# Two more query tiles transposed outside TensorE, and softmax weights divided late, in a streaming encoder step

## The chip, the cores and the metric

The kernel runs on one core of a Trainium2 chip. A core has TensorE (PE, matmuls; its weight loads are shown apart as PEld), VectorE (DVE), ScalarE (ACT), GpSimd (POOL) and SyncE (SP), which in this kernel issues every DMA, in one queue. The metric is the device time of one execution in microseconds; the median of several runs counts.

## The reference, cut to what matters

One layer of an encoder for a prompt of 1024 tokens and a sample group of 32 tokens with a cache of 512, all in float32:

```python
def finish(h, oa, ga, ob, gb, w_out, g_post, p, w_ple, w_ple_gate):
    y = jnp.concatenate([oa * jax.nn.silu(ga), ob * jax.nn.silu(gb)], axis=-1) @ w_out
    h = h + rmsnorm(y, g_post)
    return h + jax.nn.sigmoid(h @ w_ple_gate) * (p @ w_ple)

def band_attention(q, k, v, q_pos, k_pos, bias_table):      # heads A: 8 heads of 64
    s = jnp.einsum('bqhd,bkhd->bhqk', q, k).astype(jnp.float32) * ATTN_SCALE
    s = s + bias_table[:, rel]
    s = jnp.where(ok, s, NEG_INF)             # own chunk of 64 and the 8 chunks before
    w = jax.nn.softmax(s, axis=-1)
    return jnp.einsum('bhqk,bkhd->bqhd', w, v)

def stick_breaking(q, k, v, q_pos, k_pos):                  # heads B: 8 heads of 64
    z = jnp.einsum('bqhd,bkhd->bhqk', q, k).astype(jnp.float32) * ATTN_SCALE
    log_beta = jax.nn.log_sigmoid(z)
    log_1m = jnp.where(causal, jax.nn.log_sigmoid(-z), 0.0)
    after = lax.cumsum(log_1m, axis=3, reverse=True) - log_1m
    w = jnp.where(causal, jnp.exp(log_beta + after), 0.0)
    return jnp.einsum('bhqk,bkhd->bqhd', w, v)
```

Queries, keys, values and gates of both kinds come from one projection, `rmsnorm(h) @ w_in`. With s(z) the sigmoid, the weight of heads B is s(z_k) times the product of s(-z_j) over all later keys j.

## The kernel before, in words

**Precision.** A float32 operand is split in a high part, rounded to the fast matmul format, and a low part, the rest. A product takes three fast matmuls (high x high, low x high, high x low).

**Stages.** Eight head pairs are worked on in the order A0, B0, A1, B1, A2, B2, A3, B3. While one pair's attention runs, the projections of the next pair are woven in: keys, queries, values, each in three chunks of 352 tokens (24 matmuls a chunk). Beside the last pair stand the eight gate projections `gA`, `gB`. After the attention come the input embedding (`ple`), the output projection (`o0P1`, `o1P1` and so on, seven products per group of row tiles), the norm, and the last gate (`g0P1` ...). Names with `s` (`sA`, `sB`) are the sample group.

**One head.** A head has eight query tiles of 128 rows, i = 0 to 7. Tile i of heads B reads i + 1 key blocks of 128, tile i of heads A at most 5.

- `scores(i)`: two matmuls per piece of at most 512 columns write the scores to PSUM (`SA`, `SB`). In heads B a mask is added, then ScalarE writes the sigmoid of the negated scores (`om`) and the sigmoid of the scores (`be`), VectorE turns `om` into reversed running products (TENSOR_TENSOR_SCAN), and POOL multiplies both. In heads A VectorE adds the bias (read reversed) and takes the row maximum, ScalarE writes the exponentials and their sum, VectorE inverts the sum, and POOL multiplies the weights by it.
- `weights_t(i)`: the weights are turned, blocks of 128 x 128, to keys by queries. By default PE transposes them (`ptwA`, `ptwB`), ScalarE rounds the result into the high ring (`wTh`), VectorE writes the rest into the low ring (`wTl`). `ROUND` names the tiles that go another way, 4 and 6 of heads A: VectorE transposes squares of 32 x 32, one DMA stores the tile to DRAM (`swapA`), four DMAs read it back so that the squares come to their places, and rounding and subtraction run from SBUF.
- `values(g)`: for the four tiles of group g, value matmuls (`PVA`, `PVB`) accumulate in one bank, with the turned weights as the operand that is streamed; `Segments` is its access pattern, with a run of 128 elements per query tile. Low and high value parts end in different partitions; ScalarE copies one half, VectorE adds the other, and a DMA stores `ot` to `o_dr`.

**Buffers.** `om` and `be` are two rings in SBUF (`Arena`), of 3076 and 3384 columns; `wTh` and `wTl` are two more of 33 blocks. A tile of a ring waits until the earlier users of its columns are done.

**Gates.** Each of 24 gate chunks is 24 matmuls, a sigmoid on ScalarE, a product on VectorE, a product on POOL with the attention output loaded from `o_dr` (`ogg`), and a store to `og_dr`, from which the output projection loads its left sides (`uo`, `lo`). Gate buffers `sg` are three.

**Order.** Nothing is issued where it is written: `Recorder` records every operation with its dependencies, and `order` lists them by a simulation with built-in costs, engine by engine; each engine then works through its list in order. On PE the attention has the better key, and projection matmuls fill in where it is not ready. All operations are issued from one line, so the profile shows line L450 nearly everywhere, and groups are told apart by tiles.

Of the kernel before, what the change touches and what calls it, by code (L numbers as in the profile page):

```python
# [30 lines left out]
ROUND = {"A": ((4,),(6,)), "B": ()}  # L31
# [127 lines left out]
class Segments:  # L159


    def __init__(self, buf, start, step, n):
        self.buf, self.start, self.step, self.n = buf, start, step, n
        self.shape = [buf.shape[0], n, P]
        self.box = (buf.box[0], (start, start + (n - 1) * step + P))

    def get(self):
        base = self.buf.get()[:, self.start:self.start + P]
        return bass.AP(tensor=base.tensor, offset=base.offset, ap=[base.ap[0], [self.step, self.n], [1, P]])
# [83 lines left out]

class Engine:
# [9 lines left out]
class Recorder:  # L264
# [43 lines left out]
    def add(self, eng, what, args, kw):  # L308
        writes, reads = [], []
        method = what[1] if isinstance(what, tuple) else ""  # L310
        for i, a in enumerate(args):
            if isinstance(a, (View, Raw, Segments)):
                (writes if i == 0 or (method == "tensor_tensor_reduce" and i == 7) else reads).append(a)
        for k, a in kw.items():
            if isinstance(a, (View, Raw, Segments)):
                (writes if k in ("out", "accum_out") else reads).append(a)
        o = self.node(eng, what, args, kw, set())
        for mine, write in ((reads, False), (writes, True)):
            for v in mine:
                b = v.buf  # L320
                hit = False
                for other, box, wrote in b.uses:
                    if other is not o and (write or wrote) and all(p < y and x < q for (p, q), (x, y) in zip(v.box, box)):
                        o.after.add(other)
                        hit = True
# [4 lines left out]
                b.uses.append((o, v.box, write))  # L330
        o.busy, o.late = self.cost(eng, method, args, kw, writes, reads)
        o.shared = eng == "POOL"
        if eng == "DVE":
            sbuf = [v for v in reads if isinstance(v, (View, Segments)) and not v.buf.psum and v.free() > 4]
            o.shared = len(sbuf) > 1 or (method == "tensor_copy" and len(sbuf) == 1 and not writes[0].buf.psum)

    @staticmethod
    def cost(eng, method, args, kw, writes, reads):
# [3 lines left out]
        psum = any(isinstance(v, (View, Segments)) and v.buf.psum for v in reads)  # L342
# [97 lines left out]
    def emit(self, tc):  # L440
        ops = self.order()
        with tc.manual_schedule():
            for o in ops:
# [3 lines left out]
                args = [a.get() if isinstance(a, (View, Raw, Segments)) else a for a in o.args]  # L447
                kw = {k: a.get() if isinstance(a, (View, Raw, Segments)) else a for k, a in o.kw.items()}
# [7 lines left out]
def stream_step(  # L456
# [22 lines left out]
    o_dr = [scratch([P, T], f"o_dr{n}") for n in range(8)]  # L479
# [34 lines left out]
    ring0, ring1 = Arena(rec, at, "om", 3076), Arena(rec, at, "be", 3384)  # L514
    ringh, ringl = (Arena(rec, at, x, 33 * P, F32R) for x in ("wTh", "wTl"))
# [10 lines left out]
    NAMES = ["qA", "kA", "vA", "gA", "qB", "kB", "vB", "gB"]  # L526

# [14 lines left out]
    def ensure(j):  # L542
# [6 lines left out]
        if j == 2:  # L549
            pair = [ringl.tile([P, 2, 4, P], f"w{x}_{kind}{p}") for x in "hl"]  # L550
# [14 lines left out]
    def load_x(t):  # L565
        n = min(P, T - t * P)
        if t == 3:
            x34.append(at.tile([P, ringh.cols], F32, tag="wTh", name="x34")[:, 0:2 * D].rearrange("p (a c) -> p a c", a=2))
# [37 lines left out]
    def bias_rows():  # L606

        rb = ring0.tile([8, 257], "rb")
        dma(rb, rel_bias[0])
        R = ring1.tile([8, 768], "R")  # L610
# [101 lines left out]
    def col_steps(j):  # L712
# [7 lines left out]
        def mms(c, part):  # L720
# [9 lines left out]
            if k == "g" and part == 0:  # L730
                box["og"] = at2.tile([P, CH], F32, tag="bias", name=f"og{kind}{p}_{c}", bufs=2)
                dma(box["og"], o_dr[n][:, cs])
# [8 lines left out]
            if k == "g":  # L741
# [3 lines left out]
                nc.gpsimd.tensor_tensor(sg, sg, box["og"], ALU.mult)  # L745
                dma(og_dr[n, :, cs], sg)
            elif k == "q":
                nc.scalar.activation(box["st"][:, cs], acc, AF.Copy, scale=SCALE)
# [28 lines left out]

    def attention(ab, p, h):
# [5 lines left out]
        def begin():  # L784
            if ab == "A":
                bias = at2.tile([P, 640], F32, tag="bias", name=f"bias{nm}", bufs=2)
                dma(bias, bias_src(2 * p + h, P, 0, 640))
                nc.gpsimd.memset(bias[0:HD, 0:HD], NEG)
                nc.gpsimd.memset(bias[HD:P, 576:640], NEG)
# [4 lines left out]

        together = {i: g for g in ROUND[ab] for i in g}
        whole, done_with = {}, []
# [4 lines left out]
        def rooms(i):  # L801

            more = ab == "B"
            g = together.get(i, (i,))
            if g not in whole:
                n = sum(cost(x) for x in g) * P
                whole[g] = ring0.tile([P, n + more * len(g)], f"om{nm}_{i}"), ring1.tile([P, n], f"be{nm}_{i}")
            k, n = g.index(i), cost(i) * P
            a = sum(cost(x) for x in g[:k]) * P
            w0, w1 = whole[g]  # L810
            return w0[:, a + more * k:a + more * k + n + more], w1[:, a:a + n]

        def scores(i):
# [5 lines left out]
            w0, w1 = rooms(i)  # L819
# [8 lines left out]
            if ab == "B":  # L828
# [3 lines left out]
                nc.gpsimd.memset(w0[:, n:n + 1], 1.0)  # L832
                for a, b, s in pieces:
                    nc.scalar.activation(w0[:, a:b], s, AF.Sigmoid, scale=-1.0)
                for a, b, s in pieces:
                    nc.scalar.activation(w1[:, a:b], s, AF.Sigmoid)
                for a, b, s in reversed(pieces):
                    rev = w0[:, a + 1:b + 1][:, ::-1]
                    nc.vector.tensor_tensor_scan(rev, rev, s, 1.0 if b == n else w0[:, b + 1:b + 2], ALU.mult, ALU.bypass)
                nc.gpsimd.tensor_tensor(w1[:, 0:n], w1[:, 0:n], w0[:, 1:n + 1], ALU.mult)  # L840
            else:
                m = small.tile([P, 4], F32, tag="stat", name=f"stat{nm}_{i}", bufs=6)
                for j, (a, b, s) in enumerate(pieces):
                    nc.vector.tensor_tensor_reduce(
                        w0[:, a:b], s, box["bias"][:, n - b:n - a][:, ::-1], 1.0,
                        -3e38 if j == 0 else m[:, j - 1:j], ALU.add, ALU.max, m[:, j:j + 1])
                last = len(pieces) - 1
                nc.vector.tensor_scalar(m[:, 2:3], m[:, last:last + 1], -1.0, None, ALU.mult)
# [3 lines left out]
            state[i] = w0, w1  # L852

        wT = {}
# [5 lines left out]
        def weights_t(i):  # L860
            g = i // 4
            step, size = LAID[ab, g]
            if g not in wT:
                wT[g] = [x.tile([P, size * P], f"{x.name}{nm}_{g}") for x in (ringh, ringl)]
            b0 = lo_block(i)
            w0, w1 = state.pop(i)
            n = i + 1 - b0
            at_ = ((i - 4 * g) * step + b0) * P
            hi, lo = (x[:, at_:at_ + n * P] for x in wT[g])
            if i in together:  # L870

                group = together[i]
                done_with.append((i, hi, lo))
                if i != group[-1]:
                    return
                w0, w1 = whole[group]
                m = sum(cost(x) for x in group)
                first = {x: sum(cost(y) for y in group[:k]) for k, x in enumerate(group)}
                squares = w0[:, 0:m * P].rearrange("p (c b q) -> p b c q", c=4, q=32)
                for x, _, _ in done_with:  # L880
                    y = slice(first[x], first[x] + cost(x))
                    nc.vector.transpose(squares[:, y], w1[:, y.start * P:y.stop * P])
                dr = scratch([P, m * P], f"swap{nm}_{i}")
                dma(dr, w0[:, 0:m * P])
                for c in range(4):
                    x = dr[:, c * m * 32:(c + 1) * m * 32].rearrange("(g k) x -> k g x", k=32)
# [964 lines left out]
```

## Time and profile before

| | |
|---|---|
| median of 3 runs | 806.26 us (805.87 to 806.33) |
| span of the profiled execution | 802.6 us; the median is 3.7 us above it |
| PE busy | 792.0 us, 4734 matmuls |
| PEld busy | 731.4 us |
| DVE busy | 565.7 us |
| ACT busy | 539.5 us |
| POOL busy | 469.5 us |
| DMA | 146.32 MB, 61.3% of 16 engines' span |

Matmuls overlap, and their ends are modelled; the distance from one start to the next tells what a matmul costs on a full engine. In the lines by stretch the columns are PE, PEld, DVE, ACT and POOL busy time with instruction counts, the granted clock, the DMA share and GB/s. A group's line gives busy time, the mean of one in ns, and the idle time of the engine ahead of it with what ended it. A DMA group's line ends with the median time from issue to landing. In a timeline line the first number is the start, the second the time from the first start to the last end, and `x` the number of instructions merged.

### The profile page before, as it was taken

The numbers are of one execution on the slowest core, as the hardware profiler recorded it, in microseconds if no ns is written. First come the engines' busy times: TensorE is split into PE (matmuls) and PEld (weight loads), VectorE is DVE, ScalarE is ACT, GpSimd is POOL, SyncE is SP. The second block draws the span as 40 slices with busy tenths as digits, with TensorE's granted clock in tenths as the row PEclk, the third lists the DMA queues.
The fourth block names the chain that finished last, engine by engine and source line by source line (L and its number), as shares of the span: only waits on it lengthen the run. The fifth ranks groups of instructions, "written<-read, shape, count | busy, mean of one in ns | idle before, by whom it ended". The sixth has DMA issues, their size and how long they took to land.

```text
span 802.6 us, 14554 instructions
## 1 busy us (share of the span) xinstructions
PE 792.0 (99%) x4734; PEld 731.4 (91%) x4734; DVE 565.7 (70%) x1129; ACT 539.5 (67%) x1163; POOL 469.5 (58%) x554
## 2 busy tenths in 40 slices
PE   9999999999999999999999999999999999999997
PEld 7899999999999999999999899999998877888786
DVE  7627878777787888776787586854554786587655
ACT  6636787786586777776787577644437868876741
POOL 6625867795686866635473265554553448599613
PEclk9999999999999999999999999999999999999999
DMA  9419986538876565833325656344389957769634
GB/s 293 135 46 285 236 230 186 153 112 254 220 229 198 145 184 158 208 103 102 92 60 141 146 158 205 99 149 138 105 277 300 288 174 242 236 197 345 215 117 131
DMA packets 147390, 146.32 MB, mean 182 GB/s; under 512 B 37409, under 2 KB 109257, under 8 KB 147314
## 3 DMA queue, kind: packets, MB, share of 16 engines
q1 hardware_dynamic: 147314, 145.39, 61.3%
q8 instruction: 38, 0.62, 0.3%
q14 instruction: 38, 0.31, 0.1%
HBM read 90.78 MB, written 46.16 MB: 171 GB/s over the span
## 4 chain that ended last, share of the span: by engine, by line
PE 89%; DVE 3%; DMA 2%; POOL 2%; ACT 1%; issue 1%; SPq 1%; POOLq 0%; DVEq 0%; ACTq 0%
PE mm_gB L450 6%; PE mm_gA L450 6%; PE mm_kB L450 6%; PE mm_qB L450 6%; PE mm_qA L450 5%; PE mm_kA L450 5%; PE mm_vB L450 4%; PE PVB L450 4%; PE mm_vA L450 4%; PE SB L450 4%; PE ptwB L450 4%; PE SA L450 3%; PE PVA L450 3%; PE g0P L450 2%; PE g1P L450 2%; PE o1P L450 2%
## 5 line engine op out<-in xcount | busy, mean ns | idle before, releaser
L450 POOL TENSOR_TENSOR be<-be,om 128x512 f32<-128x512 f32 (+8 forms) x66 | 82.9, 1260 | 77.8 <-DVE om L450 43.9
L450 DVE TENSOR_TENSOR_SCAN om<-om,SB 128x384 f32<-128x384 f32 (+5 forms) x96 | 92.6, 968 | 21.9 <-ACT be L450 11.7
L450 POOL TENSOR_SCALAR be<-be,statA 128x640 f32<-128x640 f32 (+3 forms) x64 | 44.4, 698 | 44.4 <-DVE statA L450 35.8
L450 DVE TENSOR_TENSOR wTl<-ptwB,wTh 128x512 fp32r<-128x512 f32 (+3 forms) x96 | 50.8, 546 | 13.8 <-ACT wTh L450 12.4
L450 ACT ACTIVATE om<-SB 128x384 f32<-128x384 f32 (+5 forms) x96 | 47.4, 499 | 19.0 <-DVE SB L450 14.2
L450 ACT CAST wTh<-ptwB 128x512 fp32r<-128x512 f32 (+3 forms) x96 | 44.6, 483 | 14.5 <-PE ptwB L450 10.5
L450 ACT ACTIVATE be<-om,statA 128x640 f32<-128x640 f32 (+3 forms) x64 | 44.6, 698 | 11.2 <-DVE statA L450 9.6
L450 ACT ACTIVATE be<-SB 128x384 f32<-128x384 f32 (+5 forms) x96 | 46.8, 498 | 6.8 <-DVE om L450 6.3
L450 PE MATMUL ptwB<-ident,be 128*128 128x128 f32 x288 | 44.0, 273 | 0.1
L450 PEld LDWEIGHTS ptwB<-ident,be 128*128 128x128 f32 x288 | 34.9, 140 | 2.2 <-PE mm_vA L450 0.4
L450 DVE CUSTOM_DVE_ANT_0 om<-SA,biasA 128x320 f32<-128x320 f32 (+2 forms) x64 | 30.7, 480 | 5.3 <-PE SA L450 4.9
L450 PE MATMUL SB<-kdB,LB 128*128 128x384 f32 (+5 forms) x96 | 34.0, 357 | 0.3 <-DVE om L450 0.3
L450 ACT CAST wTh<-ptwA 128x512 fp32r<-128x512 f32 (+2 forms) x64 | 26.0, 429 | 12.0 <-PE ptwA L450 11.4
L450 DVE TENSOR_TENSOR wTl<-ptwA,wTh 128x512 fp32r<-128x512 f32 (+2 forms) x64 | 29.7, 482 | 4.9 <-ACT wTh L450 4.0
L450 PE MATMUL SB<-klB,LB 128*128 128x384 f32 (+5 forms) x96 | 32.9, 347 | 0.0
L450 PE MATMUL SA<-kdA,LA 128*128 128x320 f32 (+2 forms) x96 | 30.0, 319 | 1.1 <-DVE LA L450 0.8
L450 PE MATMUL SA<-klA,LA 128*128 128x320 f32 (+2 forms) x96 | 29.8, 319 | 0.0
L450 POOL TENSOR_TENSOR gB<-gB,gB 128x256 f32<-128x256 f32 x32 | 26.6, 848 | 0.7 <-DMA gB<-in_w_ple_gate_dram 0.4
L450 PE MATMUL ptwA<-ident,be 128*128 128x128 f32 x160 | 26.5, 274 | 0.0
L450 DVE TENSOR_TENSOR SB<-SB,maskb 128x128 f32<-128x128 f32 x64 | 18.0, 292 | 9.9 <-PE SB L450 8.0
L450 POOL TENSOR_TENSOR oB<-oB,oB 128x256 f32<-128x256 f32 x32 | 23.6, 754 | 1.4 <-DMA oB<-in_w_out_dram 1.3
L450 POOL TENSOR_TENSOR h<-h,x 128x512 f32<-128x512 f32 (+1 forms) x18 | 23.0, 1295 | 0.8 <-DVE h L450 0.8
(706 smaller groups left out, 2668.3 us busy)
## 6 DMA issues: line engine op xcount, KB each, us to landing
swapA<-om SPq DMA_DIRECT2D x16, 320.0 KB, 3.5
be<-swapA SPq DMA_DIRECT2D x64, 80.0 KB, 2.9
oB<-in_w_out_dram SPq DMA_DIRECT2D x16, 256.0 KB, 3.9
sum_dro<-oB SPq DMA_DIRECT2D x16, 256.0 KB, 2.9
gB<-in_w_ple_gate_dram SPq DMA_DIRECT2D x16, 256.0 KB, 3.7
sum_drg<-gB SPq DMA_DIRECT2D x16, 256.0 KB, 3.2
x<-in_x_prompt_dram SPq DMA_DIRECT2D x16, 256.0 KB, 4.1
h_dr<-h SPq DMA_DIRECT2D x8, 512.0 KB, 3.6
```

The lines of the kernel that those rows point to most:

```text
L450: getattr(getattr(tc.nc, o.what[0]), o.what[1])(*args, **kw)
```

## The change

- **Late division (heads A).** The exponentials stay undivided. The sums of the eight tiles of a head go into one tile `sums`, are inverted together and stored to `rs_dr`. The bias is negated and so are the queries' scale and the mask, so that the minimum can be used as the exponential's bias as it is.
- **Differences (heads B).** With running products P, the weight s(z_k) P_(k+1) is written as P_(k+1) - P_k, which holds since P_k = (1 - s(z_k)) P_(k+1). The second sigmoid goes, and POOL subtracts where it multiplied. One buffer `w` takes the place of `om` and `be`; it lies in ring `om`, now of 3776 columns, and ring `be`, now of 2600, takes the transposed squares.
- **Tiles 4 and 6 of heads B** take the way through DRAM too. The four loads now land in the low ring itself; ScalarE rounds from there into the high ring, and POOL subtracts in place (for heads A too, in which VectorE did).
- **Rings.** `wTh` and `wTl` become `Ring`, laid out as four groups of 32 columns by 33 slots, so that the landed squares are in place; the streamed operand of the value matmuls (`Span`) has runs of 32 elements. A tile, and no longer a group of four tiles, waits for the earlier users of its slots.
- **Outputs.** ScalarE copies the whole accumulator, and two DMAs store its halves to two buffers in DRAM. The gates load both, VectorE adds them, and for heads A POOL multiplies by the inverted sums, which two DMAs per chunk spread over 64 partitions each. Nine DMAs near the start write constants for the sample columns.
- `late_gate` and `AHEAD_OF` have no effect here: with `SHARE` as given no gate runs before its output.

```diff
-ROUND = {"A": ((4,),(6,)), "B": ()}
+ROUND = {"A": (4, 6), "B": (4, 6)}
+SLOTS = 33
+LOE = "P"
...
-    ring0, ring1 = Arena(rec, at, "om", 3076), Arena(rec, at, "be", 3384)
-    ringh, ringl = (Arena(rec, at, x, 33 * P, F32R) for x in ("wTh", "wTl"))
+    ring0, ring1 = Arena(rec, at, "om", 3776), Arena(rec, at, "be", 2600)
+    ringh, ringl = (Ring(rec, at, x, SLOTS) for x in ("wTh", "wTl"))
...
+    def fixed_columns():
+        x = small.tile([P, 2, NS], F32, tag="fixed", name="fixed")
+        nc.gpsimd.memset(x[:, 0], 0.0)
+        nc.gpsimd.memset(x[:, 1], 1.0)
+        for n in range(8):
+            dma(o_dr[n][1][:, SEQ:T], x[:, 0])
+        dma(rs_dr[:, SEQ:T], x[0:8, 1])
...
+    def outputs(ab, p, c):
+        cs = slice(c * CH, (c + 1) * CH)
+        x = at2.tile([P, 3, CH], F32, tag="stg", name=f"ol{ab}{p}_{c}", bufs=3)
+        for part in range(2):
+            dma(x[:, part], o_dr[sidx(ab, p)][part][:, cs])
+        if ab == "A":
+            for h in range(2):
+                row = rs_dr.real[2 * p + h:2 * p + h + 1, cs]
+                dma(x[h * HD:(h + 1) * HD, 2], Raw(rs_dr, bass.AP(tensor=row.tensor, offset=row.offset, ap=[[0, HD], [1, CH]])))
+        return x
+
+    def finish_gate(ab, sg, x):
+        GATE_ENG[0].tensor_tensor(x[:, 0], x[:, 0], x[:, 1], ALU.add)
+        if ab == "A":
+            GATE_ENG[1].tensor_tensor(x[:, 0], x[:, 0], x[:, 2], ALU.mult)
+        nc.gpsimd.tensor_tensor(sg, sg, x[:, 0], ALU.mult)
+
+    GATE_ENG = [nc.vector, nc.gpsimd]
...
                 for a, b, s in pieces:
-                    nc.scalar.activation(w0[:, a:b], s, AF.Sigmoid, scale=-1.0)
-                for a, b, s in pieces:
-                    nc.scalar.activation(w1[:, a:b], s, AF.Sigmoid)
+                    nc.scalar.activation(w[:, a:b], s, AF.Sigmoid, scale=-1.0)
                 for a, b, s in reversed(pieces):
...
-                nc.gpsimd.tensor_tensor(w1[:, 0:n], w1[:, 0:n], w0[:, 1:n + 1], ALU.mult)
+                nc.gpsimd.tensor_tensor(w[:, 0:n], w[:, 1:n + 1], w[:, 0:n], ALU.subtract)
...
-                nc.scalar.activation(w1[:, 0:n], w0[:, 0:n], AF.Exp, bias=m[:, 2:3], accum_out=m[:, 3:4])
-                nc.vector.reciprocal(m[:, 3:4], m[:, 3:4])
-                nc.gpsimd.tensor_scalar(w1[:, 0:n], w1[:, 0:n], m[:, 3:4], 1.0, ALU.mult, ALU.mult)
+                sums = box["sums"]
+                nc.scalar.activation(w[:, 0:n], w[:, 0:n], AF.Exp, bias=m[:, last:last + 1], scale=-1.0, accum_out=sums[:, i:i + 1])
+                if i == 7:
+                    nc.vector.reciprocal(sums, sums)
+                    dma(rs_dr[2 * p + h, 0:SEQ].rearrange("(i q) -> q i", q=P), sums)
...
+            if i in ROUND[ab]:
+                x = ring1.tile([P, n * P], f"x{nm}_{i}")
+                nc.vector.transpose(x.rearrange("p (c b q) -> p b c q", c=4, q=32), w[:, 0:n * P])
+                dr = scratch([P, n * P], f"swap{nm}_{i}")
+                dma(dr, x)
+                landed = f(lo).rearrange("p g s q -> p g (s q)")
                 for c in range(4):
+                    dma(landed[32 * c:32 * c + 32], dr[:, c * n * 32:(c + 1) * n * 32].rearrange("(g k) x -> k g x", k=32))
+                nc.scalar.copy(hi, f(lo))
+                (nc.gpsimd if LOE == "P" else nc.vector).tensor_tensor(lo, f(lo), f(hi), ALU.subtract)
                 return
...
-            nc.scalar.copy(ot[r], acc[o])
-            nc.vector.tensor_tensor(ot[r], acc[r], ot[r], ALU.add)
-            dma(o_dr[sidx(ab, p)][r, 4 * g * P:4 * (g + 1) * P], ot[r])
+            nc.scalar.copy(ot, acc)
+            for part, rows in enumerate((r, o)):
+                dma(o_dr[sidx(ab, p)][part][r, 4 * g * P:4 * (g + 1) * P], ot[rows])
```

More of the change, by code (lines that the diff above doesn't have):

```diff
@@ L729, in mms @@
             cs = slice(c * CH, (c + 1) * CH)
-            if k == "g" and part == 0:
-                box["og"] = at2.tile([P, CH], F32, tag="bias", name=f"og{kind}{p}_{c}", bufs=2)
-                dma(box["og"], o_dr[n][:, cs])
+            if k == "g" and part == 0 and (kind, p) not in AHEAD_OF:
+                box["og"] = outputs(ab, p, c)
             W = loaded[j]
@@ L801, in rooms @@
         def rooms(i):
[L803 to L811, printed above, removed]
+            n = cost(i) * P
+            return ring0.tile([P, n + (ab == "B")], f"w{nm}_{i}")
         def scores(i):
@@ L1184, in stream_step @@
     pairs = [("A", 0), ("B", 0), ("A", 1), ("B", 1), ("A", 2), ("B", 2), ("A", 3), ("B", 3)]
[L1185 to L1186 removed]
+    share = SHARE
+    AHEAD_OF = set()
     order = []
@@ L1193, in stream_step @@
             order += [(k + ab, p) for k in "kqv"]
-        for _ in range(share.get(n, 0)):
-            order.append(gates.pop(0))
+        for kind, q in share.get(n, ()):
+            order.append((kind, q))
+            if n < {"gA0": 3, "gA1": 3, "gB0": 4, "gB1": 4}.get(f"{kind}{q}", 7):
+                AHEAD_OF.add((kind, q))
         span.append((a, len(order)))
```

200 lines of the change are left out of this document (111 added, 89 removed).

## The prediction, made before the result

> **What bounds the kernel now.** I read the page's shares first, then the stretches of 40 us, then the chain that ended last, and only then groups and DMAs.
>
> ```profile
> span 802.6 us, 14554 instructions
> PE 792.0 (99%) x4734; PEld 731.4 (91%) x4734; DVE 565.7 (70%) x1129; ACT 539.5 (67%) x1163; POOL 469.5 (58%) x554
> PE 89%; DVE 3%; DMA 2%; POOL 2%; ACT 1%; issue 1%; SPq 1%; POOLq 0%; DVEq 0%; ACTq 0%
> PE mm_gB L450 6%; PE mm_gA L450 6%; PE mm_kB L450 6%; PE mm_qB L450 6%; PE mm_qA L450 5%; PE mm_kA L450 5%; PE mm_vB L450 4%; PE PVB L450 4%; PE mm_vA L450 4%; PE SB L450 4%; PE ptwB L450 4%; PE SA L450 3%; PE PVA L450 3%; PE g0P L450 2%; PE g1P L450 2%; PE o1P L450 2%
> ```
>
> TensorE (PE) is busy throughout and carries 89% of the chain; the transposes of B's weights (ptwB) are 4% of it. A busy PE may hide pauses, because its matmuls overlap, so I looked at where it starts what.
>
> ```profile
> 0.00:40.00 40.00, 36.97 (x210) 32.79 (x211) 28.38 (x44) 25.26 (x49) 24.51 (x46) 1.00 0.68 215
> 80.00:120.00 40.00, 39.71 (x259) 38.42 (x258) 31.86 (x86) 31.81 (x70) 28.98 (x41) 1.00 0.88 231
> 120.00:160.00 40.00, 40.00 (x260) 38.55 (x259) 32.33 (x48) 29.28 (x66) 29.37 (x37) 1.00 0.60 174
> ...
> 318.22 0.22 PE L450 MATMUL SA<-kdA,LA 128*128 128x128 f32 x1
> 318.28 0.28 PE L450 MATMUL SA<-klA,LA 128*128 128x128 f32 x1
> 318.39 0.62 PE L450 MATMUL ptwA<-ident,be 128*128 128x128 f32 x4
> 318.77 0.41 PE L450 MATMUL mm_kB<-hnl,wh_kB 128*128 128x352 f32 x1
> 319.02 0.27 PE L450 MATMUL ptwA<-ident,be 128*128 128x128 f32 x1
> 319.04 0.41 PE L450 MATMUL mm_kB<-hnl,wh_kB 128*128 128x352 f32 x1
> 319.29 1.45 PE L450 MATMUL mm_kB<-hnh,wh_kB 128*128 128x352 f32 x8
> 320.58 0.28 PE L450 MATMUL SA<-kdA,LA 128*128 128x256 f32 x1
> ```
>
> In the stretches (PE, PEld, DVE, ACT, POOL, clock, DMA share, GB/s) only the first shows PE waiting; in the attention stretches it is full while every other engine has a fifth of its time free. In the timeline eight projection matmuls start between 319.29 and 320.58, 0.161 us apart, one behind the other. So work taken off PE in the attention shortens the kernel by its start-to-start price, as long as what replaces it comes in time.
>
> **The change, part by part.**
>
> *PE.* The order of the changed program has 192 transposes in B's heads instead of 288: tiles 4 and 6 are 5 + 7 blocks in each of 8 heads, 96 transposes fewer; no other matmul is added or removed. Their price:
>
> ```profile
> L450 PE MATMUL ptwB<-ident,be 128*128 128x128 f32 x288 | 44.0, 273 | 0.1
> ```
>
> The 273 ns overlap. From 318.39 to 319.29 lie five transposes and two projection matmuls: (0.90 − 2 × 0.161) / 5 = 0.116 us each; the four starting at 318.39 alone give 0.38 / 4 = 0.095. The busy union, 44.0 / 288 = 0.153, holds overlapped tails and is the upper end. I take 0.11, between the two start-to-start readings: **96 × 0.11 = −10.6 us** (ends −9.1 and −14.7).
>
> The score matmuls at 318.22 and 318.28 start 0.06 us apart with the same 128 columns. The Trainium skill ("TensorE: Matmul & The Clock Gate", Part 1, on the 56 ns gap) gives a matmul's start-to-start distance as its columns over 2.4 GHz plus about 2.5 ns, 56 ns for 128 columns. By that rule the 96 transposes would be worth only 5.4 us and the kernel would come out some 5 us above my sum; the score pair agrees with it, the transposes of this trace do not (rival five is the same from rows).
>
> *What replaces them.* A swapped tile goes VectorE squares, store to DRAM, four loads straight into the low ring, ScalarE rounding, POOL subtraction.
>
> ```profile
> L450 DVE STREAM_TRANSPOSE om<-be 128x640 f32<-128x640 f32 x16 | 13.4, 838 | 3.1 <-POOL be L450 3.1
> swapA<-om SPq DMA_DIRECT2D x16, 320.0 KB, 3.5
> be<-swapA SPq DMA_DIRECT2D x64, 80.0 KB, 2.9
> L450 ACT CAST wTh<-be 128x640 fp32r<-128x640 f32 x16 | 11.6, 727 | 0.7 <-DMA be<-swapA 0.6
> L450 POOL TENSOR_TENSOR wl_kB<-wr_kB,wh_kB 128x512 fp32r<-128x512 f32 x8 | 12.2, 1540 | 8.1 <-ACT wh_kB L450 8.1
> L450 POOL TENSOR_TENSOR be<-be,om 128x896 f32<-128x896 f32 x8 | 14.2, 1773 | 15.2 <-DVE om L450 12.5 <-ACT Kh0sA L450 1.9 <-ACT be L450 0.8
> L450 DVE TENSOR_TENSOR_SCAN om<-om,SB 128x448 f32<-128x448 f32 x16 | 17.8, 1112 | 4.5 <-ACT be L450 2.2 <-ACT om L450 2.0
> ```
>
> For the 7-block tile from its scores on: about 1.4 of mask and sigmoids (estimate), scans 2 × 1.11, product 1.77, squares 0.84 × 1.4 = 1.2, store 3.5 × 1.4 = 4.9, four loads some 4.5, rounding 1.0, subtraction 1.54 × 1.75 = 2.7: 20 us. In the changed order PE has, between the last score matmul of tile 6 and the first value matmul of that group, between 35 and 67 us of other work in the eight B heads (14 to 45 before), counted in matmuls at these prices. So the 20 us have at least 15 us of cover for queueing; if that cover goes, the value matmuls wait and PE with them. I put 1 us for all heads (0 to 5).
>
> *The engines beside.* The second sigmoid of B (46.8 us on ScalarE), the normalising pass of A (44.4 on POOL) and the output additions on VectorE go; A's low parts move from VectorE to POOL.
>
> ```profile
> L450 ACT ACTIVATE be<-SB 128x384 f32<-128x384 f32 (+5 forms) x96 | 46.8, 498 | 6.8 <-DVE om L450 6.3 <-DVE wTl L450 0.6
> L450 POOL TENSOR_SCALAR be<-be,statA 128x640 f32<-128x640 f32 (+3 forms) x64 | 44.4, 698 | 44.4 <-DVE statA L450 35.8 <-issue 3.8 <-PE mm_vA L450 1.8
> ```
>
> None lies on the path, so none shortens it: 0. B's product becomes a difference of the same shape on POOL: 0. POOL gets in each B pair 2 × (1.9 + 2.7) = 9.2 us of low parts; over a stage of some 60 us that lifts 29.4 of 40 to about 35.5. Still free, but the least so of all engines (rival one). The ring's new layout cuts PV's operand into runs of 32 where it had runs of 128; the trace shows no such read. I take 0; a tenth more on the value matmuls, 7% of the chain, would be +5.6.
>
> *The gates.* Before, each gate piece loads one output piece; now two halves, in A also two broadcast rows of sums, with an addition on VectorE and for A a product on POOL. In the changed SP order 167 DMAs stand between the first gate weight and the last output piece (111 before). Each costs SP some 0.43 us when its lane is free.
>
> ```profile
> L450 SPq DMA_DIRECT2D be<-swapA x64: 303/430/1367, 87.2 to 482.0; - x64
> 48.80 3.88 PE mm_vA L450 x24
> 12.74 2.52 SPq L450 DMA_DIRECT2D masks<-maskb  x4
> 17.68 0.33 SPq L450 DMA_DIRECT2D x<-in_x_prompt_dram  x1
> 29.87 1.41 DVE L450 SCALAR_TENSOR_TENSOR be<-x,rs,gpre 128x512 f32<-128x512 f32 x2 [0.79 <-POOL rs L450]
> om<-in_x_prompt_dram SPq DMA_DIRECT2D x6, 512.0 KB, 5.1
> ```
>
> 167 × 0.43 = 72 us against 24 × 3.88 = 93 of gates and some 22 of attention on PE: hidden, 0 (rival two says when not).
>
> *The start.* Nine small DMAs of constants stand ahead of the load of x tile 4. At the 0.63 us of the mask copies they move it from 17.7 to 23.4; it lands 5.1 later, its square and scale take about 2, and it is used at 30.5 instead of 29.9: **+1** (0 to 5.7).
>
> *The way into the output projection.* In the changed order PE has, after the last value matmul, 13 gate matmuls (2.1 us), 56 of the input embedding and its transposes, and both P1 products, then P2, which needs B's gated outputs.
>
> ```profile
> 574.64 1.23 PE PVB L450 x8
> 576.32 29.26 PE mm_gB L450 x181
> 606.01 6.07 PE ple L450 x26
> 612.32 7.07 PE ple L450 x30
> 619.39 2.75 PE o0P L450 x12
> oggB<-o_dr SPq DMA_DIRECT2D x12, 176.0 KB, 3.6
> og_dr<-sggB SPq DMA_DIRECT2D x12, 176.0 KB, 3.3
> o_dr<-otB SPq DMA_DIRECT2D x16, 128.0 KB, 2.3
> uo<-og_dr SPq DMA_DIRECT2D x8, 256.0 KB, 5.0
> ```
>
> Cover: 2.1 + 13.6 + 5.5 = 21.2 us, where it was 49 before (575.9 to 619.39 + 2 × 2.75). The chain: copy 0.6, two stores with issue and landing 3.2, load of three pieces 3.6 plus six issues 2.6, addition 0.5, three POOL products of 1.2, store 3.3 with its issue 0.5, load of the left side 5.0, rounding 1.3: 24 us. So P2 is some **+3 us** late (0 to 9).
>
> *Sum.* 802.6 − 10.6 + 1 + 1 + 3 = 797.0 of span. The median of the three runs, 806.26, lies 3.7 above the span shown; with that **800.7**.
>
> **Rivals.**
>
> *One: POOL becomes the late engine in the first B pairs.* For it: at 35.5 of 40 a short delay is not made up, and the weights' low parts for the next projection queue behind. Against: A's stages lose 11 us of POOL work each and get 4 × 1.9 of low parts. If a third of the 9.2 us falls on PE in all but the last pair, 3 × 3.1 = +9: 809, and half of that 805.
>
> *Two, the other side: SP's queue paces the gates.* The gate's buffers are three, so a late output piece holds the sigmoid, the accumulator and then PE. Place: the last stage. At 0.69 us per DMA its 167 fill the 115 us of PE work; at 0.73 the 6 us gained are gone, and beyond it the kernel is slower. The mask copies' 0.63 speaks for it, the 0.43 median against. At 0.76: +12, 812.
>
> *Three: everything is hidden.* The tail and the start cost nothing: 802.6 − 10.6 + 3.7 = 795.7.
>
> *Four: the value matmuls read slower* in runs of 32: +5.6, 806.
>
> *Five: a transpose is worth no more than the score matmul with its 128 columns*, 0.06 us: 96 × 0.06 = 5.8 instead of 10.6, 805.5.
>
> **How the numbers follow.** This kernel's measurement tells about 0.2% from no change, 1.6 us. Chances: the forecast with its terms between their nearer ends (797 to 804.6) 0.46; rival three 0.18; rival one 0.13, over a third of it still faster; rival two 0.15; rivals four and five 0.04 each, mostly unchanged. Faster: 0.46 + 0.18 + 0.06 = 0.70; same 0.09; slower 0.21. The range reaches from a little below rival three to 811, which leaves out most of rival two; the forecast's own range is 797 to 804.6.
>
> **What would show it.** Right: B's transposes on PE number 192, PE's projection matmuls still stand 0.161 apart in the B stretches, POOL there is near 35 of 40, and PE shows one pause, of some 3 us, ahead of the second product of the output projection. Wrong: pauses of PE at value matmuls waiting for the low ring, SP issues well over half a microsecond in the gates, or a POOL above 38 of 40 between 120 and 200.

## The result, and the profile after

| | before | after |
|---|---|---|
| median | 806.19 us | 900.92 us (897.45 to 902.89) |
| ratio | | 1.116 (95% interval 1.112 to 1.120) |
| span of the profiled execution | 802.6 us | 898.6 us |
| PE busy | 792.0 us | 812.5 us |

The changed kernel is 94.7 us slower. I predicted 800.7, and the range ended at 811. The page's shares, its chain and the same stretches as before, and the output stage (PE, PEld, DVE, ACT, POOL, clock, DMA share, GB/s):

```profile
span 898.6 us, 14220 instructions
PE 812.5 (90%) x4638; PEld 740.5 (82%) x4638; DVE 539.9 (60%) x968; ACT 499.1 (56%) x1047; POOL 481.1 (54%) x536
PEclk9999969999799989989999889999997799999999
PE 75%; DMA 11%; ACT 4%; DVE 3%; POOL 3%; issue 2%; SPq 1%; POOLq 0%; DVEq 0%; ACTq 0%
...
0.00:40.00 40.00, 34.20 (x184) 30.00 (x185) 23.11 (x34) 20.99 (x41) 22.15 (x43) 0.96 0.69 214
80.00:120.00 40.00, 39.04 (x256) 38.23 (x254) 25.22 (x61) 27.22 (x59) 14.05 (x22) 1.00 0.98 192
120.00:160.00 40.00, 27.30 (x158) 26.33 (x159) 19.31 (x31) 17.70 (x38) 23.19 (x31) 0.79 0.79 190
680.00:720.00 40.00, 24.40 (x82) 17.23 (x82) 18.72 (x28) 23.45 (x44) 9.02 (x8) 0.74 1.05 354
```

PE is no longer full: DMA has 11% of the chain where it had 2%. In 120 to 160 PE was busy 40.00 of 40 before and is busy 27.30 now. Where PE pauses, the granted clock also falls (0.79, 0.74; 1.00 in every stretch shown of before), and the work behind the pause runs slower. PE's timeline shows the same four projection matmuls ahead of the pause that ends at 132.70 (0.81 us) and behind it (1.48 us):

```profile
118.23 0.81 PE L492 MATMUL mm_vB<-hnl,wh_vB 128*128 128x352 f32 x4
132.70 1.43 PE L492 MATMUL PVA<-wTh,v2A 128*128 128x512 f32 x4 [13.66 <-ACT wTh L492]
133.93 1.48 PE L492 MATMUL mm_vB<-hnl,wh_vB 128*128 128x352 f32 x4
```

So a pause costs more than its length. The mean granted clock of the whole execution is 0.949, where it was 0.999; 5% of 898.6 us is some 45 us of full-speed clock not granted (an estimate of the most that the clock can have added, since part of it falls into the pauses themselves). PE's longest waits are different ones:

```profile
PE PVA L492 <- ACT wTh L492: 15.1, 3, 13.7
PE o1P L492 <- ACT oB L492: 8.1, 2, 7.4
PE SA L492 <- DVE statA L492: 7.3, 2, 6.8
PE ple L492 <- ACT php L492: 7.3, 1, 7.3
```

(us in all, times, longest; before, no wait of PE on another engine came to more than 1.3 us.) The longest, 13.7 us up to 132.70, can be followed back in SP's timeline, the chain of that stretch and the DMA groups:

```profile
118.68 0.32 SPq L492 DMA_DIRECT2D wTl<-swapA  x1
...
119.98 0.38 SPq L492 DMA_DIRECT2D rs_dr<-sumsA  x1
...
121.71 0.84 SPq L492 DMA_DIRECT2D wTl<-swapA  x1
...
121.71 10.14 DMA wTl<-swapA
...
131.92 0.73 ACT wTh L492
...
132.70 1.43 PE PVA L492 x4
...
rs_dr<-sumsA SPq DMA_DIRECT2D x8, 4.0 KB, 12.1
wTl<-swapA SPq DMA_DIRECT2D x64, 80.0 KB, 3.8
swapB<-be SPq DMA_DIRECT2D x8, 448.0 KB, 4.7
```

The store of a head's inverted sums holds 4 KB and lands after 12.1 us in the median, where a 448 KB store of a swapped tile takes 4.7: `rearrange("(i q) -> q i")` scatters 128 x 8 values into 1024 places of 4 bytes. The load issued 1.7 us behind it lands after 10.14 us instead of the median 3.8, ScalarE rounds only then, and the value matmuls of heads A stand still. That the store holds the load up is so far only read from their order.

My first theory was therefore that these eight stores make most of the loss (T1). The rivals: the swapped tiles of heads B are late or load the queues (T2); the way into the output projection and the gates (T3).

### The profile page after: what moved, and what is told of

Same layout as the page of the kernel before. It is cut to its first block, busy times and chain, and to the rows that moved or that the text cites. A ratio compares the mean times of both kernels' runs of the same rounds, so it can differ in the third digit from the quotient of the medians.

```text
span 898.6 us, 14220 instructions
## 1 busy us (share of the span) xinstructions
PE 812.5 (90%) x4638; PEld 740.5 (82%) x4638; DVE 539.9 (60%) x968; ACT 499.1 (56%) x1047; POOL 481.1 (54%) x536
## 4 chain that ended last, share of the span: by engine, by line
PE 75%; DMA 11%; ACT 4%; DVE 3%; POOL 3%; issue 2%; SPq 1%; POOLq 0%; DVEq 0%; ACTq 0%
PE mm_gA L492 5%; PE mm_kB L492 5%; PE mm_gB L492 5%; PE mm_qA L492 5%; PE mm_vA L492 5%; PE mm_kA L492 4%; PE mm_qB L492 4%; PE PVB L492 4%; PE mm_vB L492 3%; PE SB L492 3%; PE SA L492 3%; PE PVA L492 3%; PE ptwB L492 2%; PE o3P L492 2%; PE g1P L492 2%
## 5 line engine op out<-in xcount | busy, mean ns | idle before, releaser
L492 POOL TENSOR_TENSOR om<-om 128x512 f32<-128x512 f32 (+8 forms) x66 | 75.2, 1152 | 43.8 <-DVE om L492 30.9
L492 POOL TENSOR_TENSOR wTl<-wTl,wTh 128x640 fp32r<-128x640 f32 (+1 forms) x32 | 54.6, 1711 | 14.0 <-ACT wTh L492 13.9
L492 ACT ACTIVATE om<-SB 128x384 f32<-128x384 f32 (+5 forms) x96 | 44.4, 493 | 31.2 <-DVE SB L492 18.3
L492 ACT ACTIVATE om<-om,statA 128x640 f32<-128x640 f32 (+2 forms) x64 | 44.3, 694 | 21.6 <-DVE statA L492 21.3
L492 PE MATMUL ptwA<-ident,om 128*128 128x128 f32 x160 | 27.7, 284 | 14.2 <-ACT ktB L492 5.8
L492 PE MATMUL SA<-kdA,LA 128*128 128x320 f32 (+2 forms) x96 | 32.5, 347 | 8.1 <-DVE statA L492 7.3
L492 DVE TENSOR_TENSOR wTl<-ptwA,wTh 128x512 fp32r<-128x512 f32 (+3 forms) x64 | 29.4, 485 | 16.8 <-ACT wTh L492 10.4
L492 DVE CUSTOM_DVE_ANT_0 om<-SA,biasA 128x320 f32<-128x320 f32 (+3 forms) x64 | 29.6, 484 | 15.6 <-POOL biasA L492 6.4
L492 ACT CAST wTh<-wTl 128x640 fp32r<-128x640 f32 (+1 forms) x32 | 24.7, 780 | 25.6 <-DMA wTl<-swapA 9.5
L492 ACT CAST wTh<-ptwA 128x512 fp32r<-128x512 f32 (+3 forms) x64 | 25.3, 427 | 17.7 <-PE ptwA L492 11.1
L492 PE MATMUL PVA<-wTh,v2A 128*128 128x512 f32 (+1 forms) x96 | 20.0, 332 | 15.2 <-ACT wTh L492 15.1
L492 DVE STREAM_TRANSPOSE be<-om 128x640 f32<-128x640 f32 (+1 forms) x32 | 28.8, 902 | 6.1 <-DMA swapA<-be 4.0
```

The costliest lines, as they stand in the source:

```text
L492: getattr(getattr(tc.nc, o.what[0]), o.what[1])(*args, **kw)
```

## The experiments

Differences are to the kernel before, timed beside each run on the same chip (806.0 to 806.3 us, 809.8 for the last two rows of part 7). With 2% as the yardstick for slower, ratios up to 1.016 count as the same, and 1.022 in part 7 stays unclear; but no interval given below includes 1.

**1. Without the store of the sums.** This kernel leaves the division of heads A out: the rows of sums in DRAM are ones.

```diff
-        dma(rs_dr[:, SEQ:T], x[0:8, 1])
+        o = ring1.tile([8, T], "fixedr")
+        nc.gpsimd.memset(o, 1.0)
+        dma(rs_dr, o)
...
                     nc.vector.reciprocal(sums, sums)
-                    dma(rs_dr[2 * p + h, 0:SEQ].rearrange("(i q) -> q i", q=P), sums)
```

> The changed kernel without the eight stores of the inverted sums (4 KB each in 1024 pieces of 4 bytes); the row of sums in DRAM is filled with ones at the start, so the normalisation of heads A is left out. Theory T1 (the stores hold up every DMA issued behind them on the DMA rings by some 10 us, eight times, and PE's clock falls in the pauses): 800 to 825 us. Theory T2 (the swapped tiles of heads B are too late or load the queues): 870 us or more. Theory T3 (the way into the output projection and the gates): 875 us or more, since nothing changes there but the loads of sums.

851.67 us (ratio 1.054, 1.050 to 1.058): 49 us of the loss go, 45 stay. That lies between what T1 and its rivals expect: the stores cost much, but not 80 us.

**2. The sums stored in fewer pieces.** Turned by VectorE squares, four stores of 8 rows of 128 bytes; or turned by PE, one store of 8 rows of 512 bytes:

```diff
-                    nc.vector.reciprocal(sums, sums)
-                    dma(rs_dr[2 * p + h, 0:SEQ].rearrange("(i q) -> q i", q=P), sums)
+                    pt = psum("T", f"pts{nm}")
+                    nc.tensor.transpose(pt[0:8, 0:P], sums, ident)
+                    y = ring1.tile([8, P], f"sumt{nm}")
+                    nc.vector.reciprocal(y, pt[0:8, 0:P])
+                    dma(rs_dr[2 * p + h, 0:SEQ].rearrange("(i q) -> i q", q=P), y)
```

> The changed kernel with the inverted sums first turned by VectorE squares, so that four stores of 8 rows of 128 bytes take the place of one store of 1024 pieces of 4 bytes; the values that arrive are the same. T1: 800 to 828 us, within 6 us of the run without the store, and a landing time of these stores of 2 to 4 us where it was 12.1. T2 and T3: 870 us or more.

> The changed kernel with the sums of a head turned by one PE transpose (128 x 8 to 8 x 128), inverted by VectorE on the way out of PSUM and stored by one DMA of 8 rows of 512 bytes. If the 4-byte pieces were what cost in the store: within 6 us of the run without the store, 846 to 858. If the turning and four stores of 128-byte rows cost (the run with VectorE squares, 877, stands 26 above the run without) because every additional step in heads A costs: 865 to 880.

877.36 (ratio 1.086, 1.081 to 1.091) and 870.43 us (1.079, 1.077 to 1.081): both below 900.92, both above the run without a store, by 26 and 19, not the 6 expected under T1. 870.43 lies where the other expectation put it, that any further step in heads A costs. Whether it is the step or the new order that it brings stays open; part 7 shows that a new order alone can cost as much as 19.

**3. The same store added to the kernel before**, once in 4-byte and once in 32-byte pieces (both with ring `be` 16 columns shorter):

```diff
+                if i == 7:
+                    few = small.tile([P, 8], F32, tag="few", name=f"few{nm}", bufs=2)
+                    nc.vector.tensor_copy(few, w1[:, 0:8])
+                    dma(xs_dr[2 * p + h, 0:SEQ].rearrange("(i q) -> q i", q=P), few)
# second kernel: dma(xs_dr[(2 * p + h) * P:(2 * p + h + 1) * P, :], few)
```

> The kernel before, with one more store per head A: 128 x 8 values, 1024 pieces of 4 bytes, to a place that nobody reads, issued after the last softmax of the head. T1: slower by 30 to 90 us (836 to 896), less than in the changed kernel because half as many swapped tiles wait behind the stores; the DMAs issued behind a store land some 10 us late. T2 and T3: 805 to 811 us, nobody waits for this store.

> The kernel before with the same eight extra stores of 4 KB as in the run that cost 60 us, but to 128 places of 32 bytes each instead of 1024 of 4 bytes; issued at the same point, read by nobody. If the number of pieces makes the price: 806 to 814, a landing of 2 to 4 us. If a further store at that point costs, whatever its pieces: 836 to 870.

866.16 us (+60) and 818.54 us (+12): the same bytes at the same place, 48 us apart (ratios 1.072, 1.066 to 1.077, and 1.014, 1.011 to 1.017). For the 4-byte pieces, SP's row of the store, its time to landing, PE's longest wait and ScalarE's wait for the loads of swapped tiles:

```profile
L450 SPq DMA_DIRECT2D xs_dr<-fewA x8: 366/382/440, 99.3 to 527.4; - x8
DMA to landing us min/median/max: 9.3/11.1/11.4
PE PVA L450 <- ACT wTh L450: 22.4, 6, 6.4
ACT wTh L450 <- DMA be<-swapA: 44.7, 10, 8.3
```

For the 32-byte pieces, the landing and the same wait:

```profile
DMA to landing us min/median/max: 1.4/2.1/3.3
PE PVA L450 <- ACT wTh L450: 1.7, 2, 0.9
```

The packets of the kernel before, of the 4-byte and of the 32-byte run:

```profile
DMA packets 147390, 146.32 MB, mean 182 GB/s; under 512 B 37409, under 2 KB 109257, under 8 KB 147314
DMA packets 155710, 146.36 MB, mean 170 GB/s; under 512 B 45729, under 2 KB 117577, under 8 KB 155634
DMA packets 148542, 146.36 MB, mean 179 GB/s; under 512 B 38561, under 2 KB 110409, under 8 KB 148466
```

That is 8320 and 1152 packets more, 1040 and 144 for each of the eight stores: one per piece and 16 besides. Nobody waits for this store. What is late is what stands behind it: the value matmuls of A wait 22.4 us for ScalarE, whose rounding waits 44.7 us for the loads of swapped tiles, against 1.7 us of the value matmuls with 32-byte pieces. The number of pieces makes the 48 us between the two. The +12 of the second is not shown to be the store's own: the same copies without any store cost +19 (part 7).

**4. Told to the simulation.** The simulation that writes the order reckons with less than 0.1 us for such a store (it counts runs of 8 elements, as they lie in SBUF). I told it 12 us:

```diff
+        if isinstance(args[1], View) and list(args[1].shape) == [P, 8]:
+            return ISSUE, 12000
```

> The changed kernel whole, with the simulation told that a store of the sums takes 12 us (it reckons under 0.1), so that the order lets PE do other work where the loads behind a store are late. If the stores cost because the order counts on them for nothing: 850 to 882. If the DMA rings are held up whatever the order: 890 to 905.

949.45 us (ratio 1.178, 1.171 to 1.184), 48.5 more than the changed kernel: outside both expectations. So telling the simulation their length is no remedy. The simulation has one line for all DMAs, on which 12 us now hold back every later one; that this is the reason is not shown, and what exactly makes its new order so bad was not followed up.

**5. B's tiles.** With the 4-byte stores (first) and with the sums turned by PE (second), all of B's tiles on PE; then only those of the last pair:

```diff
-ROUND = {"A": (4, 6), "B": (4, 6)}
+ROUND = {"A": (4, 6), "B": ()}
# third kernel, instead:
-            if i in ROUND[ab]:
+            if i in ROUND[ab] and (ab, p) != ("B", 3):
```

> The changed kernel with all tiles of heads B transposed by PE (288 transposes as before the change), the sums' stores as they are. T1: 890 to 915 us, the ten us of the 96 transposes given back and the stores still there. T2: 805 to 825 us.

> The same store in one DMA, and all tiles of heads B transposed by PE. If the pieces' stores (48.7 us by the run without them) and B's tiles (32.5 us by the run with B on PE) are separate costs: 815 to 825. If they share pauses, so that with one gone the other costs more: 803 to 814, as before the change. If a third part of the change costs (late division, differences, outputs in two halves, low parts on POOL): 830 or more.

> The same store in one DMA, B's tiles 4 and 6 by squares and DRAM in the first three pairs, by PE in the last pair B3. If the late way into the output projection is made by B3's swapped tiles (two PE pauses of 7.4 and 7.7 us and the lower clock behind them, in the run without the store): 20 to 28 us below the kernel with the store in one DMA, 822 to 834, and no PE pause over 2 us between 620 and 680. If B's tiles cost alike in every pair: a quarter of their cost, some 8 to 11 us, 840 to 846.

868.45 (ratio 1.075, 1.068 to 1.082), 826.05 (1.024, 1.021 to 1.027) and 845.13 us (1.048, 1.046 to 1.050). The first lies between what T1 and T2 expect, so both hold in part: the swapped tiles cost 900.92 - 868.45 = 32.5 us with the 4-byte stores and 870.43 - 826.05 = 44.4 without, and that is after the gain of 96 transposes. The last pair alone makes 870.43 - 845.13 = 25.3 of it, and the three pairs before it the other 19.1. (The ranges in us for the third kernel were set before the 870.43 of its basis was known; 845.13 lies in the wrong one of them, but the difference of 25.3 is the 20 to 28 expected of the last pair, and no quarter of 44.4.) The same two stretches with B3 swapped and with B3 on PE:

```profile
640.00:680.00 40.00, 23.80 (x99) 16.75 (x97) 15.71 (x27) 20.58 (x39) 6.28 (x6) 0.82 0.83 273
680.00:720.00 40.00, 34.39 (x132) 27.02 (x133) 27.83 (x46) 27.66 (x59) 11.04 (x8) 0.84 0.66 212
```

```profile
640.00:680.00 40.00, 40.00 (x185) 32.67 (x184) 25.66 (x42) 32.96 (x66) 15.34 (x12) 1.00 0.92 303
680.00:720.00 40.00, 40.00 (x175) 30.72 (x174) 31.54 (x53) 29.78 (x66) 25.36 (x31) 1.00 0.61 204
```

With B3 on PE no pause of PE over 2 us is left between 620 and 720. So T3 is no separate cause: the late way into the output projection comes with B3's swapped tiles. The change's longer way from the value matmuls to the gated outputs may make it worse: in the kernel before with the same tiles swapped (part 6) PE waits there once, for less than half as long as either of the two waits (7.3 for `php`, 7.4 for `oB`) of the changed kernel:

```profile
PE o1P L450 <- ACT oB L450: 3.4, 1, 3.4
```

How much each adds was not tested.

**6. Tiles of B swapped in the kernel before**, 4 and 6 in all pairs, and tile 4 alone in B0 to B2 (which I hoped would beat both):

```diff
-ROUND = {"A": ((4,),(6,)), "B": ()}
+ROUND = {"A": ((4,),(6,)), "B": ((4,),(6,))}
# second kernel: "B": ((4,),), and not in pair 3
```

> The kernel before, with tiles 4 and 6 of heads B through VectorE squares and DRAM as tiles 4 and 6 of its heads A; nothing else is changed, the low parts stay on VectorE. By the prediction's price of a transpose, with every wait hidden: 795 to 800. If B's swapped tiles are late or hold up ScalarE's and VectorE's queues: 815 to 850.

> The kernel before with tile 4 alone of heads B through squares and DRAM, in the pairs B0 to B2: 30 transposes less on PE, three other tiles between its scores and its value matmuls. If the waits are made by the short way of tile 6 and by the last pair: 802 to 805, faster than before. If the queues of ScalarE, VectorE and SP are held up by any such tile: 807 to 813.

818.71 (+12.7; ratio 1.016, 1.014 to 1.017) and 813.94 us (+7.7; ratio 1.008, 1.006 to 1.011). Taking transposes off PE brings nothing even without the rest of the change; how much of the two losses is the waits of these tiles and how much the new order (part 7) is not told apart. ScalarE loads its function tables 14 and 16 times in them, as in the kernels of part 7 in which only the order is new (14), against 8 before.

**7. What stays: 20 us.** The kernel without 4-byte stores and without swapped tiles of B is at 826.05. Two parts of the change undone in it (the nine constant stores moved to the middle of the attention; the low parts of A's tiles back on VectorE), one done alone in the kernel before (the differences of heads B), and four kernels in which next to nothing but the order changes (n2 also has ring `be` 16 columns shorter, as in part 3):

```diff
# g1:  fixed_columns() before the fourth pair, its tile in ring be
# g2:  -LOE = "P"   +LOE = "V"
# d1, in the kernel before:
-                for a, b, s in pieces:
-                    nc.scalar.activation(w1[:, a:b], s, AF.Sigmoid)
...
+                nc.gpsimd.tensor_tensor(w1[:, 0:n], w0[:, 1:n + 1], w0[:, 0:n], ALU.subtract)
# n2, in the kernel before: the copies `few` of run 3, without the store
# n4, n5, n6: before, changed, and the 826.05 kernel:
-            return 155 + 1.04 * n + (83 if method == "tensor_tensor_reduce" else 0), 0
+            return 156 + 1.04 * n + (83 if method == "tensor_tensor_reduce" else 0), 0
```

> The kernel with the sums turned by PE and B's tiles on PE (826.1), and the nine constant stores moved from the start to the middle of the attention. If they make the late start (the first score matmul begins at 70.0 us, in the kernel before near 65): 820.5 to 824, and the first score matmul at 65 to 67. If the late start has another cause: 825 to 828.

> The kernel with the sums turned by PE and B's tiles on PE (826.1), and the subtraction of the low parts of A's tiles 4 and 6 back on VectorE. If POOL's longer subtractions make part of the 20 us by which that kernel is slower than before: 812 to 822. If not: 823 to 830.

> The kernel before with the weights of heads B as differences of the running products: no second sigmoid (96 ScalarE instructions, 46.8 us, less), POOL subtracts where it multiplied. By the prediction (none of the engines beside lies on the path): 804 to 808. If any new order costs: 811 to 822, as for the kernels with next to no work added. If the differences themselves cost: above these.

> The kernel before with eight VectorE copies of 128 x 8 elements that nobody reads (some 0.2 us each) and no store: next to no work, but a new order on every engine. If the order written out anew costs by itself: 811 to 822. If the 12 us of the eight 32-byte-piece stores were the stores' own: 805 to 809.

> The kernel before with one constant of the simulation's costs changed by 1 ns (VectorE's 155 to 156): the same instructions with the same sizes in another order, nothing else. If a new order costs by itself: 811 to 822. If not: 805 to 808.

> The changed kernel whole with VectorE's cost constant in the simulation 1 ns higher (155 to 156): the same instructions in another order. If the slowdown belongs to the work: 880 to 925, the stores of sums landing after 10 to 13 us again, with PE pauses behind them. If it was an unlucky order: below 870.

> The kernel with the sums turned by PE and B's tiles on PE (826.1), the same constant 1 ns higher. If its 20 us over the kernel before are a matter of the order: anywhere from 808 to 835, more than 3 us from 826.1. If they belong to the late division, the differences and the two halves of the outputs: 823 to 829.

| kernel | median, us | to before | ratio (95%) |
|---|---|---|---|
| g1, constants later | 826.70 | +20.5 | 1.026 (1.022 to 1.030) |
| g2, low parts on VectorE | 827.58 | +21.4 | 1.025 (1.023 to 1.028) |
| d1, before with differences | 813.56 | +7.4 | 1.009 (1.007 to 1.011) |
| n2, before with eight small copies | 825.25 | +19.1 | 1.022 (1.019 to 1.025) |
| n4, before, cost + 1 ns | 811.86 | +5.7 | 1.006 (1.004 to 1.009) |
| n5, changed, cost + 1 ns | 898.34 | +88.5 | 1.111 (1.108 to 1.114) |
| n6, the 826.05 kernel, cost + 1 ns | 820.66 | +10.9 | 1.014 (1.011 to 1.017) |

Eight VectorE copies of 0.2 us in the median cost 19 us, and 1 ns in a table that never runs on the chip costs 5.7. The kernel before has an order that every edit of it tried here loses. The 20 us are about the largest of these losses and fell to 10.9 under the same 1 ns; neither constants nor low parts make them, and the differences cost no more than a new order does. That late division, halves of outputs and the new rings cost nothing of their own is not shown. The changed kernel stays near 900 under the same 1 ns, so its loss is not the accident of one order; that a third order would leave it there is not shown (part 4).

## Why the prediction was wrong

Along one chain of kernels, each against the next: +20.0 (none of the two causes, 826.05), +44.4 (B's tiles swapped, 870.43), +30.5 (sums in 4-byte pieces, 900.92). How large a part is depends on the path: the stores make 42.4 where B is on PE, 48 in the kernel before.

*The first step that failed: the store of the sums has no term.* My part "The gates" counts the two rows of sums that each chunk loads; the eight stores that write them appear nowhere, not even at 0; they make 30.5 us here, and 42 to 49 on the other paths. By the 4 KB I would have passed over them. The Trainium skill ("DMA: Bandwidth & Descriptors", Rules for kernel authors) says that a non-contiguous last dimension becomes one descriptor per element and should be rearranged; by that rule this edit spoke against itself, and the trace agrees (1040 packets a store and 12.1 us here; 144 packets and 2.1 us for 32-byte pieces). Its table in the section Bandwidth gives 0.68 us for 4 KB, for a load issued from GpSimd and as the time that the transfer is busy; for this store the measured landing decides.

*The second: cover counted in PE work.* "The 20 us have at least 15 us of cover" gave B's tiles +1; they cost 44.4, and with the predicted gain of 10.6, which is already in that, some 55 (an estimate). "The way into the output projection" gave +3; B3 makes 25.3. I set the chain against the PE matmuls that stand between, as if these could always run. They cannot: the covering matmuls need ScalarE, VectorE and POOL, which work their lists in order, and these lists wait for the same transfers. The changed kernel's ScalarE ahead of the output projection shows it:

```profile
681.83 0.62 ACT L492 CAST whA11o<-uo 128x512 fp32r<-128x512 f32 x1 [5.09 <-DMA uo<-og_dr]
684.32 0.46 ACT L492 ACTIVATE sggB<-mm_gB 128x352 f32<-128x352 f32 x1 [1.88 <-DMA og_dr<-sggB]
685.48 0.58 ACT L492 CAST php<-ptp 128x512 fp32r<-128x512 f32 x1 [0.69 <-POOL sggB L492]
```

The 56 matmuls of the input embedding, with its transposes, were 13.6 us of my cover. Their first operand `php` is rounded behind `whA11o`, which waits 5.09 us for a load of gated outputs, and behind the last gate's sigmoid, which waits for a store to free its buffer: the cover stood behind what it was to cover. PE waited 7.3 us there and 7.4 for `oB` after it, in a stretch with a clock of 0.74, for which I had no term either. For the earlier pairs, 19.1 us, the cause is argued and not shown. VectorE's list is the likely place: in the kernels with the sums turned by PE it waits 16.0 us for B's value matmuls to free the low ring where B is swapped (first), and 3.9 where B is on PE (second). In the change the loads land in that ring and so hold its slots longer.

```profile
DVE wTl L492 <- PE PVB L492: 16.0, 7, 4.9
```

```profile
DVE wTl L492 <- PE PVB L492: 3.9, 3, 3.1
```

*The third: the order was taken as given.* I priced the work that is added and taken away, as if a new order cost nothing in itself. 6 to 19 us for next to no work is as much as my four terms together (10.6, 1, 1 and 3).

*The transposes.* Right as far as it went: 192 on PE with the same mean, and successive ones still start 0.109 us apart in the median, before and after, so rival five falls. But the 10.6 us never reached the end in any run.

```profile
L492 PE MATMUL ptwB<-ident,om 128*128 128x128 f32 x192 | 29.4, 273 | 0.1
```

*The start.* +1 was predicted, 0 to 5.7 as its bounds. The first score matmul began at 65.6 us before and at 71.0 in the 826.05 kernel; with the constants moved it begins at 65.6. So +5.4, at the far end; but the total did not move (826.70), and where the gain went was not followed.

*Engines beside, gates, runs of 32.* The gates' loads took SP 0.40 to 0.47 us each in the median. POOL was busy 23.19 of 40 between 120 and 160, where I expected 35 (PE stood still there, and POOL with it), and 33.53 between 160 and 200; PE waited for POOL 0.7 us in the whole execution. The value matmuls with 512 columns start 0.235 us apart in the median in heads B, 0.233 before. Rivals one, two and four fall. Of what I had named as signs of a wrong prediction, value matmuls waiting for turned weights came true, for a reason that I had not named: all my rivals were about the parts I had priced.

## What to carry to other kernels

List every DMA that an edit adds with the number of its contiguous pieces, not its bytes, and ask what is issued behind it: a scattered store that nobody waits for delayed the loads behind it here. Cover counts only if the covering work's own inputs come from engines that aren't waiting for the same thing. Where a simulation writes the order, first change something that does no work and see how far the time moves (6 to 19 us here); no edit worth less than that can be judged by one order alone.

## What the runs showed of the hardware

*ScalarE's function tables.* The kernel before loads a function table 8 times; with eight small copies or 1 ns more it does so 14 times, 1.28 us each. In the stretch below the new order alternates between the sigmoids of heads B (from `SB`) and the exponentials of heads A (with `statA`). In the kernel with the copies (its group of loads, ScalarE's and PE's timeline) four of them stand ahead of a pause of PE of 3.64 us:

```profile
L450 ACT ACT_TABLE_LOAD x14 | 18.0, 1283 | 1.0 <-PEq L1842 0.7
...
477.34 1.28 ACT L450 ACT_TABLE_LOAD   x1
478.63 0.28 ACT L450 ACTIVATE om<-SB 128x128 f32<-128x128 f32 x1
479.41 1.28 ACT L450 ACT_TABLE_LOAD   x1
480.70 0.83 ACT L450 ACTIVATE be<-om,statA 128x640 f32<-128x640 f32 x1
481.97 1.28 ACT L450 ACT_TABLE_LOAD   x1
483.26 0.28 ACT L450 ACTIVATE be<-SB 128x128 f32<-128x128 f32 x1
483.83 1.28 ACT L450 ACT_TABLE_LOAD   x1
...
486.68 0.80 PE L450 MATMUL SB<-kdB,LB 128*128 128x512 f32 x1 [3.64 <-DVE om L450]
```

The four loads lie on the chain that leads to this pause: one way in which an order costs. It is not that of the changed kernel and of the 826.05 kernel, which load 8 times too.

*VectorE shut out by POOL.* In the kernel with the 32-byte stores a VectorE instruction with two SBUF operands (TENSOR_TENSOR) stood 8.06 us while POOL ran its own such instructions back to back, against 1.79 us in the kernel before (first the former, POOL's last lines below it); PE paused 2.5 us for its successors. The 826.05 kernel shows the same, 8.09.

```profile
739.24 8.06 DVE L450 TENSOR_TENSOR gT<-raw,gT 128x512 fp32r<-128x512 f32 x1
740.42 1.32 POOL L450 TENSOR_TENSOR gT<-raw,gT 128x512 fp32r<-128x512 f32 x1
741.67 1.32 POOL L450 TENSOR_TENSOR gB<-raw,gB 128x512 fp32r<-128x512 f32 x1
742.92 1.33 POOL L450 TENSOR_TENSOR cc2P<-cc2P,hh 128x512 f32<-128x512 f32 x1
744.18 2.58 POOL L450 TENSOR_TENSOR gB<-raw,gB 128x512 fp32r<-128x512 f32 x2
```

```profile
728.85 1.79 DVE L450 TENSOR_TENSOR gT<-raw,gT 128x512 fp32r<-128x512 f32 x1
```

The Trainium skill ("SBUF — State Buffer", Who interferes with whom) says that a VectorE instruction with two SBUF inputs and a POOL instruction that reads SBUF contend for a shared port pair, an exclusive lock. The trace fits with that, though no run takes these POOL instructions away; but here VectorE waited past five instruction boundaries of POOL. Why the wait ended at the first boundary in the kernel before and not here was not tried.
